# A diffusion trunk on one core: GpSimd's elementwise instructions go to VectorE

## The chip, the cores and the metric

The kernel runs on 1 core of one Trainium2 chip. The metric is device time in microseconds of one execution. Times before are given as the median of three runs. Engines: TensorE (PE, with PEld for its weight loads), VectorE (DVE), ScalarE (ACT), GpSimd (POOL) and SyncE (SP, here a queue for DMAs).

## The reference

Four layers over two streams of 256 tokens, a context (half 0) and a latent (half 1), D = 1024. The mixers are a gated linear attention (layers 0 and 3), a neighbourhood attention (layer 1) and an S5 state space (layer 2). Each layer does twice: norm, scale and shift by a vector computed from a condition, a mixer or a convolutional FFN, norm, scale, add to the residual. In the last layer only the latent goes on.

```python
for i in range(DEPTH):
    h = rmsnorm(x, norm_g[i, 0]) * (1.0 + m[1]) + m[0]
    x = x + m[2] * rmsnorm(mixer(h), norm_g[i, 1])
    h = rmsnorm(x, norm_g[i, 2]) * (1.0 + m[4]) + m[3]
    x = x + m[5] * rmsnorm(conv_ffn(h, ...), norm_g[i, 3])
```

## The kernel before

Activations lie transposed: eight tiles of 128 features (index k) by 256 tokens for each half. Matmuls are done in three passes over two parts of each operand: `mm3` (L688 to L690) multiplies the high part of the weights with the high and the low part of the input, and the low part of the weights with the high input. So each weight tile is split into `whi` (ScalarE, L112) and `wlo` (VectorE, L115), and each input into a high half (ScalarE, L574) and a low half, computed value minus high half.

There is no planner: each engine works off its instructions in the order in which the code emits them. Work beside the matmuls sits in Python generators that are advanced by `tick()` between matmuls; a `yield` in a generator sets what is emitted next. `drain()` runs all generators to their end with nothing in between.

**The step between stages** is `chain(l, n, half, nxt)`, called 14 times: after mixer (n = 1) or FFN (n = 3) of each layer, for each half. First it takes the square sums of y, which `sum_mm` (L446) broadcasts through a matmul with ones; `rstd_sb` takes the root on ScalarE (L460) and the reciprocal on VectorE (L462), named `bc`; in the last step `bc` is a ScalarE copy (L469) and `bp` the same values in PSUM, elsewhere both names are one SBUF tile. Then the residual loop over k: y times g times `bp` (L520, VectorE) and x plus y (L526, VectorE). For the k listed in `tp`, GpSimd has first multiplied y by `bc` (L517), and one VectorE instruction does the rest (L524). ScalarE squares the new x (L530) for the next norm. For the second half, and at the entry of S5, this loop is emitted in one burst; elsewhere it yields after each k.

After the second reciprocal the loop over k makes the next input: t = x times g times `bc` (L561, VectorE), the high half on ScalarE (L574), the low half on VectorE (L581), emitted with a delay of three entries (`HL`). For the k in `HP[half]` ScalarE writes the full value once more (L577) and GpSimd subtracts the high half (L578). This is done in 11 of the chains; at the entry of S5 there is no split.

**Square sums of the first half.** `sq_add` squares on ScalarE (L484). For half 0 `sq_sum` adds the squares of k = 2 to 6 elementwise onto two tiles (L476) so that fewer sums go through TensorE; k = 2 and 4 on GpSimd, the others on VectorE. After attention `outtail` copies y out of PSUM (L827 or L825) and calls `sq_add` for each of the eight tiles, with weight splits between; in the FFN the y tiles come one at a time (L980).

**S5 preparation.** `s5_prep` runs as a generator beside the FFN of layers 0 and 1, eight iterations each. Its `outer` makes two complex outer products: two products on VectorE (L1480), two on GpSimd into `Wt` (L1479), combined on VectorE (L1483, L1485); the result W goes to DRAM, or to TensorE for transposes (L1538). In front of the FFN's output, ScalarE and VectorE apply the convolution (L883, L886, L887), which frees the PSUM bank, and the gate (L892 to L895).

GpSimd's queue also issues the weight loads of the S5 mixer (L1555).

Of the kernel before, what the change touches and what calls it, by code (L numbers as in the profile page):

```python
# [19 lines left out]
FHEAD, FTAIL = (2, 1)  # L20
DM = 1
CW = (1, 8, 6)
HP = ((1, 3, 5), (1, 3, 5))
FT = (2, 6)
DF = 1
AE = (1, 1)
# [13 lines left out]
WB = 4  # L40
ORDER = '00 10 m 01 m f1 l 11 m 20 m 21 f2 30 m 31 m 40 f3 41 s 50 51 60 61 70 71'
TL = 1
TP = ((1, 3, 5, 7), (1, 3, 5, 7), (3, 6))
CF = (3, 2)
C0 = 3
ET = (0, 1)
# [24 lines left out]
MUL, ADD, SUB, MAX = ALU.mult, ALU.add, ALU.subtract, ALU.max  # L71
# [80 lines left out]
class Kern:  # L152
# [319 lines left out]
    def sq_sum(self, key, k, q):  # L472
        st = self.pst.setdefault(key, {})
        if 1 < k < 7:
            a = st[k % 2]
            (self.nc.vector if k % 2 or k == 6 else self.nc.gpsimd).tensor_tensor(a, a, q, op=ADD)  # L476
        else:
            st[k] = q

# [12 lines left out]
    def chain(self, l, n, half, nxt):  # L492
# [3 lines left out]
        if n is not None:  # L496
# [17 lines left out]
            g = lambda k: self.g1[:, l, n, k, half:half + 1]  # L514
            tp = TP[half if half or n == 1 and KINDS[l] != 2 else 2]
            for k in tp:
# [40 lines left out]
        for k in range(NK):  # L557
# [14 lines left out]
            else:  # L572
                hi, lo = self.hh[:, half, k], self.hl[:, half, k]
                nc.scalar.activation(hi, t, AF.Identity, bias=m, scale=1.0)  # L574
                if k in HP[half]:
                    h = self.np_.tile([128, 256], F32, name="sq", bufs=2)
# [882 lines left out]
    def s5_prep(self, p, i0, i1):  # L1459
        nc = self.nc  # L1460
# [11 lines left out]
        def outer(pw, br, bi, neg):  # L1472
            W = p.tile([128, 4, 2, 8, 16], F32, name="W", bufs=2)
            P = lambda i: pw[:, i, :, :, None].to_broadcast([128, 4, 8, 16])
            B = lambda x: x[:, :, None, :].to_broadcast([128, 4, 8, 16])
            v, g = nc.vector, nc.gpsimd
            for u, (x, y) in enumerate(((br, bi), (bi, br))):
                t = p.tile([128, 4, 8, 16], F32, name="Wt", bufs=1)
                g.tensor_tensor(t, P(1), B(y), op=MUL)  # L1479
                v.tensor_tensor(W[:, :, u], P(0), B(x), op=MUL)  # L1480
                yield
                if u and neg:
                    v.scalar_tensor_tensor(W[:, :, u], W[:, :, u], -1.0, t, op0=MUL, op1=SUB)  # L1483
                else:
                    v.tensor_tensor(W[:, :, u], W[:, :, u], t, op=ADD if u else SUB)  # L1485
            return W

        nxt = load(i0)
        for it in range(i0, i1):
# [10 lines left out]
            nc.vector.tensor_scalar(ncim, bc[:, 3, :4], -1.0, None, op0=MUL)  # L1500
            yield
            W = yield from outer(pw[:, 1], bc[:, 2, :4], bc[:, 3, :4], True)
            nc.sync.dma_start(self.Gd[it], W.rearrange("p g i s c -> p g i (s c)"))
            yield
            W2 = yield from outer(pw[:, 0], bb[:, 0, :4], bb[:, 1, :4], False)
            ps = self.aux()
            psb = self.aux()
# [25 lines left out]
            for h in range(2):  # L1533
                yield
                ps = self.aux()
                for u in range(4):
                    q, i = 2 * h + u // 2, u % 2
# [392 lines left out]
```

## Time and profile before

| | |
|---|---|
| median of three runs | 2921.64 us (2917.19 to 2922.3) |
| the profiled execution | 2920.22 us |
| its span, first to last instruction | 2918.4 us |
| mean granted TensorE clock | 0.969 |
| TensorE busy | 2740.2 us (94%) |
| VectorE busy | 1992.1 us (68%) |
| ScalarE busy | 1290.1 us (44%) |
| GpSimd busy | 194.9 us (7%), 192 instructions |

The span is what the profile covers; the metric holds 1.8 us more. Busy is the time in which an instruction of the engine was running; matmuls overlap, so TensorE's busy share isn't its share of its peak. The granted clock is 1.0 at 2.4 GHz and 0.5 at 1.2 GHz. An instruction's duration can overlap with that of the next one on its engine.

### The profile page before, as it was taken

How to read it: one execution, taken by the hardware profiler on the slowest of the kernel's cores; microseconds unless marked ns; L12 is line 12 of the kernel's file. 1: busy time of each engine (PE TensorE's matmuls, PEld its weight loads, DVE VectorE, ACT ScalarE, POOL GpSimd, SP SyncE). 2: the span in 40 equal slices, each digit the busy share in tenths (PEclk: the TensorE clock that was granted, in tenths of full speed). 3: DMA queues.
4: the chain of work that ended last, by engine and by line, in shares of the span. 5: the costliest groups of instructions: out<-in, count | busy, mean ns of one | idle time of the engine just before them, and what ended most of it. 6: DMA issues, size and time to landing. Idle time of an engine off the chain costs nothing.

```text
span 2918.4 us, 53174 instructions
## 1 busy us (share of the span) xinstructions
PE 2740.2 (94%) x21814; PEld 2267.2 (78%) x21814; DVE 1992.1 (68%) x4405; ACT 1290.1 (44%) x2154; POOL 194.9 (7%) x192
## 2 busy tenths in 40 slices
PE   8999998999999999899999877989999989998998
PEld 5787776877788777777777745778888877887998
DVE  5775768766557655687564766378687876777776
ACT  4333334634335545553333565454332463433554
POOL 0000001122101000012110010010000010000000
PEclk9999999999999999999999988899999999999999
DMA  6232232355524343235555387433334453332553
GB/s 260 88 112 93 102 99 76 131 178 178 172 93 150 104 164 109 102 123 191 199 180 178 125 228 251 150 120 132 137 124 147 143 179 126 120 124 95 186 182 124
DMA packets 127043, 421.26 MB, mean 144 GB/s; under 512 B 36048, under 2 KB 55760, under 8 KB 102096
## 3 DMA queue, kind: packets, MB, share of 16 engines
q1 hardware_dynamic: 118608, 391.64, 39.5%
q0 software_dynamic: 5472, 23.07, 2.3%
q8 instruction: 172, 2.82, 0.4%
q10 hardware_dynamic: 2720, 3.15, 0.3%
q14 instruction: 71, 0.58, 0.1%
HBM read 392.78 MB, written 29.23 MB: 145 GB/s over the span
## 4 chain that ended last, share of the span: by engine, by line
PE 72%; DVE 16%; ACT 5%; DMA 3%; issue 2%; SPq 1%; POOL 0%; ACTq 0%; DVEq 0%; POOLq 0%
PE acc L688 19%; PE acc L689 18%; PE acc L690 17%; DVE wlo L115 3%; PE aux L314 2%; PE aux L1103 2%; PE acc L724 2%; PE acc L726 1%; PE acc L725 1%; DVE bc L462 1%; DVE y L561 1%; ACT whi L112 1%; PE aux L1143 1%; PE aux L383 1%; DVE y L520 1%
## 5 line engine op out<-in xcount | busy, mean ns | idle before, releaser
L688 PE MATMUL acc<-h,whi 128*128 128x512 f32 (+1 forms) x2368 | 868.3, 367 | 24.8 <-ACT h L574 15.3
L689 PE MATMUL acc<-h,whi 128*128 128x512 f32 (+1 forms) x2368 | 842.7, 356 | 19.4 <-DVE h L581 17.0
L690 PE MATMUL acc<-h,wlo 128*128 128x512 f32 (+1 forms) x2368 | 837.8, 354 | 2.3 <-DVE wlo L115 2.3
L115 DVE TENSOR_TENSOR wlo<-wraw,whi 128x512 fp32r<-128x512 f32 (+5 forms) x674 | 601.7, 920 | 153.0 <-ACT whi L112 152.6
L688 PEld LDWEIGHTS acc<-h,whi 128*128 128x128 f32 x2368 | 458.6, 194 | 94.1 <-ACT h L574 18.2
L689 PEld LDWEIGHTS acc<-h,whi 128*128 128x128 f32 x2368 | 458.9, 194 | 80.0 <-DVE h L581 24.3
L112 ACT ACTIVATE whi<-wraw 128x1024 fp32r<-128x1024 f32 (+3 forms) x496 | 479.5, 1014 | 66.6 <-PE acc L689 51.7
L690 PEld LDWEIGHTS acc<-h,wlo 128*128 128x128 f32 x2368 | 458.8, 194 | 62.1 <-DVE wlo L115 3.2
L688 PE MATMUL acc<-gh,whi 128*128 128x256 f32 (+1 forms) x872 | 294.7, 338 | 8.6 <-ACT gh L894 8.6
L689 PE MATMUL acc<-gl,whi 128*128 128x256 f32 (+1 forms) x872 | 287.2, 329 | 0.8 <-DVE gl L895 0.7
L690 PE MATMUL acc<-gh,wlo 128*128 128x256 f32 (+1 forms) x872 | 287.1, 329 | 0.0
L883 ACT ACTIVATE u<-acc,vec 128x512 f32<-128x512 f32 (+1 forms) x190 | 129.6, 692 | 254.5 <-PE acc L690 254.3
L886 DVE SCALAR_TENSOR_TENSOR u<-acc,vec,u 128x510 f32<-128x510 f32 (+1 forms) x190 | 122.2, 643 | 113.2 <-ACT u L883 113.0
L688 PEld LDWEIGHTS acc<-gh,whi 128*128 128x128 f32 x872 | 164.8, 189 | 25.6 <-ACT gh L894 9.0
L689 PEld LDWEIGHTS acc<-gl,whi 128*128 128x128 f32 x872 | 164.7, 189 | 16.8 <-DVE gl L895 1.7
L690 PEld LDWEIGHTS acc<-gh,wlo 128*128 128x128 f32 x872 | 164.6, 189 | 15.9
L1074 DVE TENSOR_TENSOR FB<-FB,P 128x256 f32<-128x256 f32 x384 | 145.2, 421 | 31.9 <-PE aux L1103 29.3
L887 DVE SCALAR_TENSOR_TENSOR u<-acc,vec,u 128x510 f32<-128x510 f32 (+1 forms) x190 | 123.1, 648 | 6.7
L724 PE MATMUL acc<-whi,h 128*128 128x256 f32 x384 | 115.2, 300 | 2.2 <-ACT whi L112 1.2
L894 ACT ACTIVATE gh<-u 128x512 fp32r<-128x512 f32 (+1 forms) x95 | 52.3, 551 | 144.1 <-DVE u L893 144.1
L726 PE MATMUL acc<-wlo,h 128*128 128x256 f32 x384 | 110.0, 287 | 4.1 <-DVE wlo L115 4.1
L725 PE MATMUL acc<-whi,h 128*128 128x256 f32 x384 | 109.7, 286 | 0.0
(298 smaller groups left out, 3957.2 us busy)
## 6 DMA issues: line engine op xcount, KB each, us to landing
wm<-in_w_mod SPq DMA_DIRECT2D x192, 512.0 KB, 5.3
wraw<-in_f_w_in SPq DMA_DIRECT2D x89, 1024.0 KB, 4.9
wraw<-in_fo SPq DMA_DIRECT2D x44, 896.0 KB, 4.6
wraw<-in_a_qz SPq DMA_DIRECT2D x18, 1024.0 KB, 4.9
wraw<-in_a_zg SPq DMA_DIRECT2D x18, 1024.0 KB, 4.9
wraw<-in_fo SPq DMA_DIRECT2D x16, 1024.0 KB, 4.9
wraw<-in_a_v SPq DMA_DIRECT2D x15, 1024.0 KB, 4.9
wraw<-in_c_glu SPq DMA_DIRECT2D x12, 1024.0 KB, 4.8
```

Source lines behind the costliest of these rows:

```text
L112: nc.scalar.activation(hi[:, a:b], r[:, a:b], AF.Copy)
L115: nc.vector.tensor_tensor(lo[:, a:b], r[:, a:b], hi[:, a:b].bitcast(F32), op=SUB)
L688: nc.tensor.matmul(ps, wh[:, k], hh, start=(first and k == 0), stop=False, **kw)
L689: nc.tensor.matmul(ps, wh[:, k], hl, start=False, stop=False, **kw)
L690: nc.tensor.matmul(ps, wl[:, k], hh, start=False, stop=(last and k == nk - 1), **kw)
L724: nc.tensor.matmul(o, hh, wh[:, :, k, :], start=(k == 0), stop=False)
L725: nc.tensor.matmul(o, hl, wh[:, :, k, :], start=False, stop=False)
L726: nc.tensor.matmul(o, hh, wl[:, :, k, :], start=False, stop=(k == NK - 1))
L883: nc.scalar.activation(u, ps[c], AF.Identity, scale=w(1), bias=self.vec[:, cb0 + ch:cb0 + ch + 1])
L886: nc.vector.scalar_tensor_tensor(u3[:, :, 1:], p3[:, :, :255], w(0), u3[:, :, 1:], op0=MUL, op1=ADD)
L887: nc.vector.scalar_tensor_tensor(u3[:, :, :255], p3[:, :, 1:], w(2), u3[:, :, :255], op0=MUL, op1=ADD)
L1074: nc.vector.tensor_tensor(o, o, p, op=MUL)
```

## The change

All elementwise instructions of GpSimd go to VectorE. The lists `HP` and `TP` become empty: every low half is made by L581 (and ScalarE's second copy, L577, is not emitted), every residual product by L520 followed by L526. The square adds of k = 2 and 4 and the S5 products go to VectorE at the places in the code where GpSimd did them. GpSimd keeps its DMA issues and one memset. Nothing else is touched.

```diff
@@ -20,7 +20,7 @@
-HP = ((1, 3, 5), (1, 3, 5))
+HP = ((), ())
@@ -40,7 +40,7 @@
-TP = ((1, 3, 5, 7), (1, 3, 5, 7), (3, 6))
+TP = ((), (), ())
@@ -473,7 +473,7 @@
         if 1 < k < 7:
             a = st[k % 2]
-            (self.nc.vector if k % 2 or k == 6 else self.nc.gpsimd).tensor_tensor(a, a, q, op=ADD)
+            self.nc.vector.tensor_tensor(a, a, q, op=ADD)
         else:
             st[k] = q
@@ -1473,7 +1473,7 @@
             B = lambda x: x[:, :, None, :].to_broadcast([128, 4, 8, 16])
-            v, g = nc.vector, nc.gpsimd
+            v = g = nc.vector
             for u, (x, y) in enumerate(((br, bi), (bi, br))):
                 t = p.tile([128, 4, 8, 16], F32, name="Wt", bufs=1)
                 g.tensor_tensor(t, P(1), B(y), op=MUL)
```

## Rows read from the trace of the kernel before

**Rows 1.** The page: busy times, and the chain that ended last by engine.

```profile
PE 2740.2 (94%) x21814; PEld 2267.2 (78%) x21814; DVE 1992.1 (68%) x4405; ACT 1290.1 (44%) x2154; POOL 194.9 (7%) x192
...
PE 72%; DVE 16%; ACT 5%; DMA 3%; issue 2%; SPq 1%; POOL 0%; ACTq 0%; DVEq 0%; POOLq 0%
```

**Rows 2.** Groups by line, GpSimd: count | busy us, mean ns | idle before, releasers.

```profile
L1479 POOL TENSOR_TENSOR Wt<-pw,bb 128x512 f32<-128x512 f32 x32 | 46.7, 1459 | 100.3 <-DVE W L1485 61.0 <-DVE W L1483 39.3
...
L517 POOL TENSOR_TENSOR y<-y,bc 128x256 f32<-128x256 f32 x48 | 42.0, 902 | 611.5 <-DVE bc L462 407.8 <-ACT bc L469 203.6
L578 POOL TENSOR_TENSOR h<-sq,h 128x256 fp32r<-128x256 f32 x33 | 27.9, 846 | 160.6 <-ACT sq L577 160.1 <-POOL h L578 0.5
L476 POOL TENSOR_TENSOR sq<-sq,sq 128x256 f32<-128x256 f32 x12 | 10.4, 868 | 1383.2 <-ACT sq L484 1383.2
```

**Rows 3.** Durations of one line, L520: min/median/max ns.

```profile
L520 DVE SCALAR_TENSOR_TENSOR y<-y,g,bc x60: 470/478/1069, 473.9 to 2693.6; 128x256 f32<-128x256 f32 x60
```

**Rows 4.** Timeline, VectorE, 498 to 522 us: start, us, line, count.

```profile
498.38 2.50 DVE L115 TENSOR_TENSOR wlo<-wraw,whi 128x512 fp32r<-128x512 f32 x4 [0.34 <-ACT whi L112]
...
502.70 1.06 DVE L520 SCALAR_TENSOR_TENSOR y<-y,g,bc 128x256 f32<-128x256 f32 x1
...
508.87 0.48 DVE L524 SCALAR_TENSOR_TENSOR x<-y,g,x 128x256 f32<-128x256 f32 x1
...
513.96 1.67 DVE L561 SCALAR_TENSOR_TENSOR y<-x,g,bc 128x256 f32<-128x256 f32 x4
```

**Rows 5.** Timeline, GpSimd, the same stretch.

```profile
502.74 3.34 POOL L517 TENSOR_TENSOR y<-y,bc 128x256 f32<-128x256 f32 x4 [6.17 <-DVE bc L462]
```

**Rows 6.** Timelines, VectorE and TensorE, 2680 to 2712 us (layer 3).

```profile
2700.94 1.67 DVE L561 SCALAR_TENSOR_TENSOR y<-x,g,bc 128x256 f32<-128x256 f32 x4
...
2706.37 1.26 DVE L581 SCALAR_TENSOR_TENSOR h<-y,mT,h 128x256 fp32r<-128x256 f32 x3
...
2690.98 1.14 PE L446 MATMUL aux<-y,ones 128*128 128x256 f32 x2 [4.72 <-ACT y L530]
2692.71 5.85 PE L446 MATMUL aux<-y,ones 128*128 128x256 f32 x14 [0.59 <-ACT y L530]
...
2705.23 0.58 PE L689 MATMUL acc<-h,whi 128*128 128x256 f32 x1 [0.92 <-DVE h L581]
```

**Rows 7.** Timeline, VectorE, 1212 to 1275 us (after layer 1's attention).

```profile
1212.38 1.41 DVE L827 TENSOR_TENSOR y<-acc,y 128x256 f32<-128x256 f32 x4
1214.34 0.72 DVE L476 TENSOR_TENSOR sq<-sq,sq 128x256 f32<-128x256 f32 x1 [0.54 <-ACT sq L484]
```

**Rows 8.** Timelines, VectorE and TensorE, at the entry of S5.

```profile
1651.24 1.94 DVE L520 SCALAR_TENSOR_TENSOR y<-y,g,bc 128x256 f32<-128x256 f32 x2
...
1659.18 0.41 DVE L476 TENSOR_TENSOR y<-y 128x256 f32<-128x256 f32 x1
...
1663.94 0.58 PE L688 MATMUL acc<-gh,whi 128*128 128x256 f32 x1 [8.20 <-ACT gh L894]
```

**Rows 9.** Timeline, TensorE, in the S5 preparation: the longest wait for W.

```profile
588.00 0.55 PE L1538 MATMUL aux<-ident,W 128*128 128x128 f32 x3 [1.85 <-DVE W L1485]
```

**Rows 10.** Timeline, VectorE, the last residual step, first and last row.

```profile
2909.77 0.48 DVE L520 SCALAR_TENSOR_TENSOR y<-y,g,aux 128x256 f32<-128x256 f32 x1 [1.28 <-ACT bc L469]
...
2914.79 0.47 DVE L524 SCALAR_TENSOR_TENSOR x<-y,g,x 128x256 f32<-128x256 f32 x1
```

**Rows 11.** Timelines, TensorE, at transitions: waits that end on these steps.

```profile
506.86 3.82 PE L446 MATMUL aux<-y,ones 128*128 128x256 f32 x14 [1.03 <-ACT y L530]
...
904.60 0.70 PE L446 MATMUL aux<-sl,ones 128*128 128x256 f32 x2 [1.37 <-ACT sl L484]
...
1698.49 1.12 PE L1644 MATMUL acc<-ident,vt 128*64 128x128 f32 x8 [3.23 <-ACT vt L1637]
...
1922.81 0.39 PE L690 MATMUL acc<-h,wlo 128*128 128x256 f32 x1 [0.96 <-DVE wlo L115]
```

**Rows 12.** Stretches: us, busy us (count) by engine, PEclk, DMA share, GB/s.

```profile
560.00:740.00 180.00, 177.93 (x1154) 139.20 (x1153) 120.58 (x212) 69.84 (x109) 35.50 (x25) 0.99 0.51 174
```

## Prediction

> **What bounds the kernel now.** The page's busy times and its chain that ended last say that TensorE is the bound: 94% busy, 72% of the chain [rows 1]. VectorE has 16% of the chain, so more VectorE work can cost time, but only where TensorE waits for it. GpSimd has 0% of the chain and 7% of the span. Read alone, that says that its work is hidden and that moving it to a busier engine can only lose.
>
> The groups of instructions by line, GpSimd only, give the pieces that move [rows 2]: 64 S5 products at up to 1.46 us (two groups of 32; the longer stands), 48 residual products (902 ns), 33 low halves (846 ns) and 20 square adds (two groups; the twelve on the sq tiles stand, 868 ns). Next the durations of the VectorE line that does the same step as L517: 470 ns at least, 478 median, but 1069 at most [rows 3]. The timeline shows which are long. In the residual burst at 502 us GpSimd runs from 502.74 for 3.34 us [rows 5]; the VectorE instruction that starts at 502.70 takes 1.06 us and the one at 508.87, after GpSimd has ended, 0.48 [rows 4]. Both have the same size and both read two SBUF tensors. This is what the case turns on: while GpSimd computes, VectorE instructions there run at half speed. GpSimd has no time of its own on the chain, but it lengthens VectorE's.
>
> Last, TensorE's own idle times: which of them end on a chain of VectorE work. They stand at the transitions between stages [rows 6, 8, 9, 11, 12].
>
> **Prices.** From start to start a scalar_tensor_tensor of 128x256 takes (1.67 - 0.48)/3 = 0.40 us [rows 4]; a tensor_tensor (1.41 - 0.41)/3 = 0.33 us [rows 7, 8], both on data that GpSimd doesn't touch at that time; a tensor_tensor of 128x512 2.50/4 = 0.63 us at most [rows 4]. The last one of a run adds 0.08. The added low half, residual product and square add are such instructions, and the S5 product has the shape of the wlo row, with broadcast inputs; its bounds are 0.63 and, by GpSimd's row, 1.46 [rows 2], and I take 0.63, the same engine. VectorE gains 64 x 0.63 + 48 x 0.40 + 33 x 0.40 + 20 x 0.33 = 79 us of issue time; ScalarE loses 33 copies (L577, counted below at nothing, since VectorE paces those stretches).
>
> **A. Low halves (HP, 11 chains of three).** Before, VectorE issues 8 L561 and 5 L581; in layer 3 from 2700.94 to 2706.37 + 1.26 = 2707.63, so 6.69 us [rows 6]. After, 16 instructions without GpSimd: 16 x 0.40 + 0.08 = 6.4 us. The end gains 0.3, but TensorE waits earlier: it stood 0.92 us until 2705.23 for the low half of k=2 [rows 6]. In the code the order becomes t0 to t3, lo0, t4, lo1, t5, lo2, t6, lo3, t7, lo4. lo2 is the ninth instruction and ends 9 x 0.40 + 0.08 = 3.7 us after 2700.94; before, TensorE was released after 4.29. lo4 is the thirteenth, 5.3 us; before it was the first of the three at 2706.37 and ended after 5.9. So the halves that TensorE waits for come 0.6 sooner, and ScalarE's spared copies don't stand ahead of its own. I take 0.8 per chain, bounds 0.3 (the last half) and 1.3 (0.92 of idle and the 0.3): 11 x 0.8 = **8.8 us**, 3.3 to 14.
>
> **B. Residual bursts of the second half (TP, four products each).** Before: 502.70 to 508.87 + 0.48 = 6.65 us [rows 4], with 12 VectorE instructions. After: 8 x 0.40 + 8 x 0.33 + 0.08 = 5.9. Gain 0.73. TensorE waits for the squares of these rows (1.03 us at 506.86 [rows 11]) in three chains of this form: 2.2. In layer 3 the sums start 4.72 us late [rows 6]; row 0 is ready after two scalar_tensor_tensor and one tensor_tensor, 0.7 sooner, and row 1 sooner still by 1.7, so the 0.59 us before 2692.71 go as well: 1.3. At the entry of S5, TensorE waits 3.23 us for a ScalarE copy that stands behind those squares [rows 11]; up to 1.7, nothing if the S5 loads set the pace; I take 1.2. Two chains (near 935 and 2365 us) have other work between: 0 and 0.6. Sum **5.3 us**, 2 to 8.
>
> **C. Residual steps of the first half.** Entry of S5: one burst, 1651.24 to 1659.18 + 0.41 = 8.35 us, ending in TensorE's longest stall there, 8.20 us [rows 8]. After: 16 instructions and five adds, 8 x 0.40 + 13 x 0.33 + 0.08 = 7.6: 0.75. In the two FFN tails before layers 1 and 3 TensorE waits 1.37 us behind two L520 that take 1.94 together instead of 0.88 [rows 8, 11]: 0.7 each after the two added adds. At 1922.81 a wlo split stands behind such a pair, 0.96 us [rows 11]: 0.9.
> Against it: after attention, sq_add's adds come in VectorE's order between the copies of y. Each waits 0.54 us for its ScalarE square before it runs [rows 7]; two more such waits cost 2 x (0.54 + 0.33) = 1.7, less 2 x 0.3 for adds no longer slowed (0.72 there), so 1.1 late at the reciprocal, and the copies and weight splits behind them are late too. Then row 0 is ready 0.7 sooner, and the two products at k = 5 and 7 cost 2 x 0.40 where VectorE has no idle time. So 1.1 - 0.7 + 0.8 = 1.2 lost in each of two chains. In FFN tails TensorE is busy for longer than those waits: nothing; if that cover is gone, 8 adds x 0.87 = 7 us. Sum: 0.75 + 1.4 + 0.9 - 2.4 = **0.65 us**, -7 to 3.
>
> **D. The last residual step.** There bp is read from PSUM, and L520 isn't slowed (0.48). From 2909.77 to 2914.79 + 0.47 = 5.49 us [rows 10]; after 5.9. **0.4 us lost**, on the path to the last store.
>
> **E. S5 products.** They fall in the FFN stages of layers 0 and 1. In 560 to 740 us VectorE is busy 120.6 of 180 us and TensorE 177.9 [rows 12]. 25 of GpSimd's instructions there, at most 25 x 0.63 = 16 us more on VectorE, leave some 43 free. TensorE's stalls there are waits for W, the longest 1.85 us [rows 9], because VectorE waited for the product on GpSimd; with 0.63 in place of 1.46 this one and three shorter ones mostly go: **2 us**, 0 to 3.
>
> Sum: 8.8 + 5.3 + 0.65 - 0.4 + 2 = 16.3 us of the profiled execution's 2920.2 (span 2918.4, and 1.8 around it): 2903.9. That execution lies 1.4 us below the median, so 2905.3. The clock is taken as unchanged: the idle that lowers it between stages mostly stays.
>
> The burst of part B bears on a rule of the Trainium skill: four L561 take 1.67 us, though one lasts 0.48 [rows 4], so an instruction starts before the one before it has ended. "VectorE: DVE Perf Modes", section "The DRAIN you can't avoid", says that the next instruction doesn't start until the pipe is empty, though it allows an earlier start for one that isn't held. By the plain rule part B would lose and part A too; by the row both gain, and the row is of this kernel.
>
> **Rivals.**
> *Absorbed.* TensorE's sums, weight splits and ScalarE take the place of each wait. Then only the last halves (11 x 0.3), layer 3 (1.3), S5's burst (0.75) and half of E count: 6.4 - 0.4 - 2.4 = 3.6 us, 2918. For it: at the transitions TensorE also waits for ScalarE and weights. Against: the rows of 6, 8 and 11 end on exactly the slowed instructions. Within 0.2% (about 5.8 us, what a measurement of this kernel can tell from no change). 0.20.
> *VectorE becomes the bound in the S5 preparation (slower).* Each product sits in front of the convolution step that frees a PSUM bank. If every one held TensorE up by its 0.63: 64 x 0.63 = 40 us, and with A to D gaining 14, 2947. It decides from about 0.22 us per product. Against it: the 43 us free [rows 12], and four banks. 0.08; a typical case 2935.
> *Durations add up.* If added instructions cost their duration rather than the spacing, a burst takes 8 x 0.48 + 8 x 0.41 = 7.1 against 6.65, seven of them +3; the low halves 16 x 0.48 = 7.7 against 6.69, 11 x 1.0 = +11; D 7.1 - 5.49 = +1.6; C about +5 (the 2.4 stays, 0.8 at S5, 0.5 in each of three tails); E still -2: 19 us slower, 2940. The spacing rows speak against it. 0.06. (It is what the skill's rule named above would give.)
>
> **How the numbers follow.** Forecast 0.66, absorbed 0.20, the two slower cases 0.14. Likeliest 2905.3; its own range is 2894 (every upper bound at once, 28 us) to 2916 (where no change begins). The whole range, 2893 to 2923, takes in the absorbed case and leaves out the slower ones. Faster 0.66, same 0.20, slower 0.14.
>
> **What the profile after should show.** GpSimd left with the S5 loads alone; L520, L561, L581 and L526 without any at 0.9 us or more; the burst at about 5.9 us, the low halves at 6.4; TensorE's waits for low halves shorter, those for W nearly gone; the reciprocal after attention in layers 0 and 1 about 1 us late; the last step 0.4 longer. Wrong it would be if VectorE's instructions stay long without GpSimd, if they start only when the one before has ended, or if TensorE shows new waits for u or wlo in 560 to 740 us.

## The result, and the profile after

The changed kernel takes 2899.95 us (median of four runs, 2897.44 to 2904.39) against 2920.56 us for the kernel before beside it: ratio 0.9933, 95% interval 0.9919 to 0.9947, or 19.6 us less (15 to 24; the ratio is that of the means, the medians differ by 20.6). Forecast were 16.3 us less, 2905.3 us. The profiled execution has a span of 2898.8 us and a mean granted clock of 0.975.

The page after, with the lines of [rows 1]: busy times, and the chain by engine.

```profile
PE 2730.3 (94%) x21814; PEld 2255.8 (78%) x21814; DVE 2014.8 (70%) x4570; ACT 1281.6 (44%) x2121; POOL 15.5 (1%) x27
...
PE 71%; DVE 18%; ACT 5%; DMA 3%; issue 2%; SPq 1%; POOL 0%; ACTq 0%; DVEq 0%; POOLq 0%
```

VectorE executes 165 more instructions and is busy only 22.7 us longer. Issue time of 79 us was added, so the rest must have become shorter. Two views show it: the durations of L520 (ns, min/median/max), which answers to [rows 3], and the groups of VectorE by line and shape.

```profile
L520 DVE SCALAR_TENSOR_TENSOR y<-y,g,bc x104: 475/480/490, 476.6 to 2676.6; 128x256 f32<-128x256 f32 x104
```

```profile
L561 DVE SCALAR_TENSOR_TENSOR y<-x,g,bc 128x256 f32<-128x256 f32 x104 | 46.5, 480 | 1.1
L526 DVE TENSOR_TENSOR x<-x,y 128x256 f32<-128x256 f32 x112 | 46.4, 421 | 0.0
L581 DVE SCALAR_TENSOR_TENSOR h<-y,mT,h 128x256 fp32r<-128x256 f32 x88 | 39.6, 481 | 0.0
L476 DVE TENSOR_TENSOR sq<-sq,sq 128x256 f32<-128x256 f32 x30 | 12.8, 425 | 15.4 <-ACT sq L484 15.4
L1479 DVE TENSOR_TENSOR Wt<-pw,bb 128x512 f32<-128x512 f32 x32 | 22.1, 690 | 0.8
```

No residual or low-half instruction takes 0.9 us or more. The last two rows are moved work: an add that took 868 ns on GpSimd takes 425, a product that took 1459 takes 690 [rows 2].

VectorE's timeline has the residual burst of [rows 4] (first and last row), the low halves of layer 3 [rows 6] and the last residual step [rows 10].

```profile
504.16 0.88 DVE L520 SCALAR_TENSOR_TENSOR y<-y,g,bc 128x256 f32<-128x256 f32 x2
...
509.33 0.76 DVE L526 TENSOR_TENSOR x<-x,y 128x256 f32<-128x256 f32 x2
...
2682.51 1.67 DVE L561 SCALAR_TENSOR_TENSOR y<-x,g,bc 128x256 f32<-128x256 f32 x4
...
2687.27 1.67 DVE L581 SCALAR_TENSOR_TENSOR h<-y,mT,h 128x256 fp32r<-128x256 f32 x4
...
2889.80 0.87 DVE L520 SCALAR_TENSOR_TENSOR y<-y,g,aux 128x256 f32<-128x256 f32 x2 [1.28 <-ACT bc L469]
...
2894.94 0.76 DVE L526 TENSOR_TENSOR x<-x,y 128x256 f32<-128x256 f32 x2
```

The burst takes 5.93 us (forecast 5.9), the low halves 6.43 (6.4), the last step 5.90 (5.9). TensorE's timeline shows what it still waits for: in layer 3, at the entry of S5 and in the S5 preparation ([rows 6, 8, 9, 11] before).

```profile
579.05 0.62 PE L1510 MATMUL aux<-W,bb 64*32 64x112 f32 x24 [1.21 <-DVE W L1483]
...
587.30 0.55 PE L1538 MATMUL aux<-ident,W 128*128 128x128 f32 x3 [1.66 <-DVE W L1485]
...
1655.88 0.58 PE L688 MATMUL acc<-gh,whi 128*128 128x256 f32 x1 [8.02 <-ACT gh L894]
...
1689.00 0.66 PE L1644 MATMUL acc<-ident,vt 128*64 128x128 f32 x8 [1.58 <-ACT vt L1637]
...
2673.54 6.59 PE L446 MATMUL aux<-y,ones 128*128 128x256 f32 x16 [4.03 <-ACT y L530]
...
2686.21 0.58 PE L689 MATMUL acc<-h,whi 128*128 128x256 f32 x1 [0.17 <-DVE h L581]
```

The wait for the low half of k = 2 shrank from 0.92 to 0.17 us, and its matmul starts 3.70 us after the first L561 of the loop (4.29 before, forecast 3.7). Also shorter are the start of layer 3's sums, from 4.72 to 4.03, and the wait for vt, from 3.23 to 1.58. The 8.20 us stall lost only 0.18, and the waits for W stand.

**Where the 19.6 us came from.** Busy and idle time of TensorE (idle is span less busy), with a second profile of either kernel (below) in brackets: busy 2740.2 (2742.7) before and 2730.3 (2733.0) after, idle 178.2 (177.3) and 168.5 (166.5). In this account half of the gain is less idle time, and half is that the same 21814 matmuls took 10 us less. The number of matmuls is the same, so the second half is put down to the clock: its mean over the executions is 0.9680 in 43 of the kernel before (0.965 to 0.971) and 0.9722 in five of the changed one (0.970 to 0.975).

The account is not yet a price of the clock, since a TensorE that computes faster also waits more (last section). Executions at an equal clock tell more: with 0.970 or 0.971 the kernel before took 2915.3 us on average (eight executions, 2913.9 to 2917.2), the changed one 2900.3 (three, 2897.4 to 2904.4). So some 15 us of the gain are there without a higher clock, and about 5 go with it. With three executions on one side this is an estimate.

### The profile page after: what moved, and what is told of

It is laid out like the page before. It is cut to its first block, busy times and chain, and to the rows that moved or that the text cites. A ratio compares the mean times of both kernels' runs of the same rounds, so it can differ in the third digit from the quotient of the medians.

```text
span 2898.8 us, 52998 instructions
## 1 busy us (share of the span) xinstructions
PE 2730.3 (94%) x21814; PEld 2255.8 (78%) x21814; DVE 2014.8 (70%) x4570; ACT 1281.6 (44%) x2121; POOL 15.5 (1%) x27
## 4 chain that ended last, share of the span: by engine, by line
PE 71%; DVE 18%; ACT 5%; DMA 3%; issue 2%; SPq 1%; POOL 0%; ACTq 0%; DVEq 0%; POOLq 0%
PE acc L688 18%; PE acc L689 17%; PE acc L690 17%; DVE wlo L115 3%; PE aux L314 2%; PE aux L1103 2%; ACT whi L112 2%; PE acc L724 2%; PE acc L726 1%; PE acc L725 1%; DVE bc L462 1%; PE aux L1143 1%; PE aux L383 1%; DVE y L520 1%; DVE y L561 1%
## 5 line engine op out<-in xcount | busy, mean ns | idle before, releaser
L115 DVE TENSOR_TENSOR wlo<-wraw,whi 128x512 fp32r<-128x512 f32 (+5 forms) x674 | 591.2, 905 | 147.8 <-ACT whi L112 147.6
L688 PEld LDWEIGHTS acc<-h,whi 128*128 128x128 f32 x2368 | 453.6, 192 | 94.0 <-ACT h L574 19.1
L689 PEld LDWEIGHTS acc<-h,whi 128*128 128x128 f32 x2368 | 453.2, 191 | 73.0 <-DVE h L581 19.0
```

Of the source, the lines that this page charges most:

```text
L115: nc.vector.tensor_tensor(lo[:, a:b], r[:, a:b], hi[:, a:b].bitcast(F32), op=SUB)
L688: nc.tensor.matmul(ps, wh[:, k], hh, start=(first and k == 0), stop=False, **kw)
L689: nc.tensor.matmul(ps, wh[:, k], hl, start=False, stop=False, **kw)
```

## The experiments

**One part alone.** Theory: while a GpSimd instruction runs, VectorE's instructions with two SBUF inputs take twice as long, so every part that leaves GpSimd gains by itself. Rivals: other waits absorb it; one part is everything. Each kernel is the one before with one part of the change:

```diff
e1_low:  -HP = ((1, 3, 5), (1, 3, 5))
         +HP = ((), ())
e2_res:  -TP = ((1, 3, 5, 7), (1, 3, 5, 7), (3, 6))
         +TP = ((), (), ())
e3_sq:   -(self.nc.vector if k % 2 or k == 6 else self.nc.gpsimd).tensor_tensor(a, a, q, op=ADD)
         +self.nc.vector.tensor_tensor(a, a, q, op=ADD)
e4_s5:   -v, g = nc.vector, nc.gpsimd
         +v = g = nc.vector
```

> The kernel before with the low halves alone moved (HP empty, 33 of them, and ScalarE's 33 second copies gone); the residual products, square adds and S5 products stay on GpSimd. Theory (GpSimd's instructions lengthen VectorE's, so each part that takes them away gains by itself): 8.8 us less, 3.3 to 14. Rival 'absorbed' (TensorE's other waits take the place): about 3 us less. Rival 'one part carries all': nearly the whole 20.6 us or nothing.

> The kernel before with the residual products alone moved (TP empty, 48 of them). Theory: the bursts and residual steps gain 5.3 + 0.75 + 1.4 + 0.9 and lose 0.4, about 8 us less, of which up to 1.6 may be lost again where VectorE has no idle time after attention; 4 to 11. Timeline: the S5 entry should begin its first sums about 3.8 us sooner against its reciprocal, as it does with all parts moved. Rival 'absorbed': 2 us less or none.

> The kernel before with the 20 square adds alone moved. Theory: each moved add makes VectorE wait for its ScalarE square, so the reciprocals after attention in layers 0 and 1 come later; 2 us more in time (0 to 4). Rival (fewer GpSimd instructions always help): 1 to 2 us less, since the VectorE adds beside them are no longer slowed (0.72 down to 0.41 us).

> The kernel before with the 64 S5 products alone moved. Theory: 2 us less (0 to 3), by the waits for W and by the L115 splits and convolution steps that are no longer slowed. If the layer 0 FFN's gain of some 3 us and the loss of some 2 us in layer 1's FFN, which the two traces show between reciprocals, belong to these products, both show here without the other parts. Rival: the products hold TensorE up in the S5 preparation, 5 us more or worse.

| kernel | ratio to before (95%) | us | mean clock |
|---|---|---|---|
| e1_low | 0.9952 (0.9937 to 0.9967) | -14.0 | 0.9720 |
| e2_res | 0.9952 (0.9935 to 0.9969) | -14.0 | 0.9713 |
| e3_sq | 1.0002 (0.9992 to 1.0012) | +0.6 | 0.9694 |
| e4_s5 | 0.9995 (0.9986 to 1.0005) | -1.5 | 0.9701 |

Low halves and residual products carry the gain, each with more than was forecast for it. For square adds and S5 products no gain or loss can be told from none; the intervals also leave room for the 2 us that were forecast for either. One expectation fell: the gain of the layer 0 FFN is not that of the S5 products alone. Between the reciprocals (L462) at 512.11 and 899.69 us the changed kernel gains 3.1 us, e1_low 3.1, e2_res 2.7 and e4_s5 1.7.

**Both main parts, and ScalarE's copies.** The two gains add up to 28 us, more than the whole change has. e9_lowres is before with `HP` and `TP` empty. e8_copies tests what part A's gain is made of: the spared copies of L577 come back into the changed kernel, used by nobody.

```diff
                 nc.scalar.activation(hi, t, AF.Identity, bias=m, scale=1.0)
+                if k in (1, 3, 5):
+                    h = self.np_.tile([128, 256], F32, name="sq", bufs=2)
+                    nc.scalar.activation(h, t, AF.Identity, bias=m, scale=1.0)
```

> The kernel before with the low halves and the residual products moved (HP and TP empty), the square adds and the S5 products left on GpSimd. Alone these two parts gave ratios of 0.9952 each. Theory 'each gain is its own' (the stalls that each removes are different ones): ratio about 0.990, 28 us less, which beats the changed kernel by some 8 us, since square adds and S5 products gave nothing alone. Rival 'the two share a gain' (the profiles show that part of it is fewer stretches at 1.2 GHz, and one edit can be enough to keep the clock up): about 0.993, 20 us less, the same as the changed kernel.

> The changed kernel with ScalarE's 33 second copies (L577, k = 1, 3, 5 of each low-half loop) emitted again, used by nobody. Theory (VectorE paces the low halves, so the spared copies were worth nothing, as counted in the prediction): ratio stays near 0.993. Rival (part A's gain is that ScalarE's high halves come sooner because the copies don't stand ahead of them): about 8 us of the gain go, ratio near 0.996, and TensorE waits for high halves in those stages.

e9_lowres: 0.9933 (0.9921 to 0.9946), 2900.57 us, mean clock 0.9716. The rival holds: 0.990 lies outside the interval, and the two parts share a gain of 8 or 9 us. From the three intervals that shortfall is known only to 1 to 16 us (an estimate). e8_copies: 0.9943 (0.9931 to 0.9956), 2901.56 us; the rival's 8 us would be 0.9960, just above the interval, and losses up to 6 us are not excluded. TensorE's first wait for a high half in layer 3 is 2.46 us with and without the copies, so the trace gives the rival no support.

What is shared can be seen in the stretches (us, busy us and count by engine, PEclk, DMA share, GB/s) from 515 to 530, 900 to 985 and 1195 to 1275 us. First the kernel before in its second profile (e10_before), then the changed kernel; in the same stretch the kernels are up to 7 us apart in their work.

```profile
515.00:530.00 15.00, 13.57 (x100) 12.07 (x100) 13.26 (x27) 11.85 (x24) 2.47 (x3) 0.89 0.22 70
900.00:985.00 85.00, 75.81 (x496) 64.65 (x495) 59.81 (x109) 40.88 (x87) 12.36 (x14) 0.90 0.35 128
1195.00:1275.00 80.00, 67.49 (x422) 57.81 (x423) 65.63 (x122) 45.04 (x97) 13.27 (x16) 0.90 0.26 93
```

```profile
515.00:530.00 15.00, 14.30 (x117) 12.75 (x117) 13.38 (x32) 11.65 (x23) 0.00 (x0) 1.00 0.21 71
900.00:985.00 85.00, 77.31 (x537) 65.97 (x537) 62.14 (x132) 44.09 (x90) 0.00 (x0) 0.96 0.35 119
1195.00:1275.00 80.00, 69.55 (x464) 59.30 (x463) 63.34 (x129) 45.35 (x91) 0.00 (x0) 0.96 0.24 83
```

The same stretches in e1_low, and then in e2_res:

```profile
515.00:530.00 15.00, 14.31 (x118) 12.78 (x117) 13.27 (x32) 11.29 (x23) 0.00 (x0) 1.00 0.21 71
900.00:985.00 85.00, 76.39 (x530) 65.62 (x529) 62.61 (x123) 43.48 (x89) 7.12 (x8) 0.96 0.33 118
1195.00:1275.00 80.00, 68.34 (x467) 59.77 (x466) 64.69 (x121) 44.88 (x92) 8.39 (x10) 0.96 0.25 83
```

```profile
515.00:530.00 15.00, 13.61 (x110) 12.34 (x103) 13.37 (x27) 11.89 (x25) 2.52 (x3) 1.00 0.21 71
900.00:985.00 85.00, 76.10 (x515) 64.74 (x514) 59.88 (x119) 45.26 (x95) 7.78 (x8) 0.94 0.34 118
1195.00:1275.00 80.00, 69.11 (x461) 59.10 (x461) 63.43 (x123) 47.04 (x96) 6.38 (x8) 0.95 0.25 83
```

At 515 us the clock stays up if either part is done, and the second part can't raise it again. In the other two stretches either part alone lifts it from 0.90 to between 0.94 and 0.96, where the changed kernel has 0.96 (0.94 and 0.98 in its second profile). At 515 us e2_res still has the waits for low halves (0.45 and 0.57 us by TensorE's timeline) and yet keeps 1.00. Where it falls is seen in e10_before, TensorE:

```profile
925.64 0.39 PE L689 MATMUL acc<-h,whi 128*128 128x256 f32 x1 [0.66 <-DVE h L581]
...
927.79 0.58 PE L689 MATMUL acc<-h,whi 128*128 128x256 f32 x1 [0.93 <-DVE h L581]
928.16 0.41 PE L690 MATMUL acc<-h,wlo 128*128 128x256 f32 x1
928.38 0.41 PE L688 MATMUL acc<-h,whi 128*128 128x256 f32 x1
928.59 0.42 PE L689 MATMUL acc<-h,whi 128*128 128x256 f32 x1
```

After waits of 0.62, 0.66 and 0.93 us, the last of which ended 3.2 us after the first, each matmul takes 0.21 us from start to start instead of 0.12: 1.2 instead of 2.4 GHz. The changed kernel's profile shows 0.61, 0.66 and 0.51, then three waits of 0.17 to 0.18 us there, and the matmuls stay at 0.12.

**GpSimd runs, and nobody needs it.** These two tell contention apart from waiting for GpSimd's results. Both are the changed kernel, with useless work on GpSimd beside the residual loops (48 places), the low halves (33) and the square adds (20); VectorE never waits for it. The S5 products have no such counterpart, and line numbers behind the new function are 6 and 8 higher (L526 and L528 are L520, L532 is L526).

```diff
e6_dummy, and e7_memset with the lines of the second half instead:
+    def idle(self, src):
+        gd = self.np_.tile([128, 256], F32, name="gd", bufs=1)
+        self.nc.gpsimd.tensor_tensor(gd, src, src, op=MUL)

+        self.nc.gpsimd.tensor_copy(gd[:, :1], src[:, :1])
+        for _ in range(3):
+            self.nc.gpsimd.memset(gd, 0.0)
```

> The changed kernel, with GpSimd computing products that nobody uses (128x256, reading SBUF) at the same places as before: 48 beside the residual loops, 33 beside the low halves, 20 beside the square adds; VectorE waits for none of them. Theory (a running GpSimd instruction halves the speed of VectorE's two-input instructions): instructions of 0.9 to 1.1 us are back on L520, L526, L561 and L581, and the time goes back to that of the kernel before or above it, ratio 0.998 to 1.008. Rival (what was lost was VectorE's wait for GpSimd's results and the hand-over between the engines): L520 and L561 stay at 0.48 us, ratio stays near 0.993.

> As the run with unused products, but each replaced by three memsets of 128x256 on GpSimd (about 0.8 us together, an estimate from the memset rows of the trace), which write SBUF and read nothing, with a copy of one column ahead that waits for the same tile. Theory, by the Trainium skill, page SBUF — State Buffer, section Who interferes with whom (only a GpSimd instruction that reads SBUF holds VectorE up): durations stay at 0.48 us and the ratio near 0.993. Rival (any running GpSimd instruction that touches SBUF slows VectorE): as with the products, ratio 0.998 or more.

e6_dummy: ratio 1.0067 (1.0053 to 1.0080), 2937.12 us. e7_memset: 0.9935 (0.9923 to 0.9948), 2899.98 us. First e6_dummy, VectorE in the burst that ran in 5.93 us above, and GpSimd beside it; then the durations of e6_dummy's and of e7_memset's copy of L520.

```profile
507.74 1.24 DVE L526 SCALAR_TENSOR_TENSOR y<-y,g,bc 128x256 f32<-128x256 f32 x2
508.90 0.83 DVE L532 TENSOR_TENSOR x<-x,y 128x256 f32<-128x256 f32 x1
509.65 0.83 DVE L526 SCALAR_TENSOR_TENSOR y<-y,g,bc 128x256 f32<-128x256 f32 x1
510.41 0.83 DVE L532 TENSOR_TENSOR x<-x,y 128x256 f32<-128x256 f32 x1
511.16 0.47 DVE L526 SCALAR_TENSOR_TENSOR y<-y,g,bc 128x256 f32<-128x256 f32 x1
```

```profile
507.85 3.10 POOL L474 TENSOR_TENSOR gd<-bc 128x256 f32<-128x256 f32 x4 [7.11 <-DVE bc L462]
```

```profile
L526 DVE SCALAR_TENSOR_TENSOR y<-y,g,bc x104: 468/476/840, 477.3 to 2711.6; 128x256 f32<-128x256 f32 x104
```

```profile
L528 DVE SCALAR_TENSOR_TENSOR y<-y,g,bc x104: 474/479/487, 474.4 to 2676.3; 128x256 f32<-128x256 f32 x104
```

Long instructions are back, with 0.83 us here and 0.90 at most on the four lines (0.9 to 1.1 were expected), and end with GpSimd's last product at 510.95. VectorE is busy 2049.4 us, 34.6 more than after for the same 4570 instructions, which is 0.34 us for each of the 101 products. The span is 36.2 us longer, and the clock in the three stretches above is back at 0.89 to 0.90. e7_memset keeps GpSimd busy for longer (172.1 us against 93.4) and changes nothing. So what was lost was not the wait for a result, and not that GpSimd runs or writes SBUF. What the products do and the memsets don't is to read SBUF. The Trainium skill, page "SBUF — State Buffer", section "Who interferes with whom", says the same: a VectorE instruction with two SBUF inputs contends with a GpSimd instruction that reads SBUF, and not with one that only writes it. The trace agrees in the bursts (0.83 against 0.42 us); in the last step of e6_dummy it doesn't (last section).

**Second profiles, and the square adds back.** e10_before and e11_after repeat the two kernels without an edit. e5_sqback is the changed kernel with the line of e3_sq as it was before.

> The kernel before once more, unchanged, for a second profile. The two profiles differ in TensorE's mean granted clock, 0.969 before and 0.975 after. Theory (the change removes stalls, and the clock falls less often as a consequence): the clock comes out at 0.968 to 0.971 again, TensorE's busy time at 2738 to 2742 us. Rival (where the clock falls differs from one execution to the next by as much as between the kernels): clock up to 0.975, busy time down to 2730.

> The changed kernel once more, unchanged, for a second profile. Theory (fewer low-clock stretches belong to the change): clock 0.974 to 0.976, TensorE's busy time about 2730 us, idle about 168. Rival (chance): clock down to 0.970, busy time up to 2738, with idle time smaller by as much, since a TensorE that computes slower waits less.

> The changed kernel with the square adds of k = 2 and 4 back on GpSimd, nothing else. Theory (on VectorE each of them waits for its ScalarE square, which makes the reciprocals after attention late): the reciprocals at 475 and 1218 us come 1 to 2 us sooner against the work before them, and the time is 2 us less, ratio 0.992 to 0.993. Rival (GpSimd's adds slow the weight splits and y's residual steps beside them by as much): 2 us more, ratio 0.994.

e10_before: 2921.81 us, clock 0.967. e11_after: 2901.51 us, clock 0.974. Both lie nearer to their own kernel's first profile than to the other's, although e10_before falls just below the 0.968 that was expected. By the means the kernel decides on the clock more than chance does, but single executions scatter by 0.0015 to 0.002, and two of e3_sq reach 0.973 and 0.974, so one profile can't show it. e5_sqback: 0.9927 (0.9914 to 0.9941), 2898.23 us, which is not told apart from the changed kernel; in the trace the place is plain. VectorE of the changed kernel, then of e5_sqback, from the last reciprocal of the attention (L426) to that of the chain (L462):

```profile
460.29 0.17 DVE L426 RECIPROCAL rs<-rs 128x2 f32<-128x2 f32 x1 [0.47 <-ACT rs L425]
...
464.31 0.42 DVE L476 TENSOR_TENSOR sq<-sq,sq 128x256 f32<-128x256 f32 x1 [0.48 <-ACT sq L484]
...
474.86 1.75 DVE L462 RECIPROCAL bc<-aux 128x256 f32<-128x256 f32 x1
```

```profile
458.67 0.17 DVE L426 RECIPROCAL rs<-rs 128x2 f32<-128x2 f32 x1 [0.48 <-ACT rs L425]
459.40 0.56 DVE L115 TENSOR_TENSOR wlo<-wraw,whi 128x384 fp32r<-128x384 f32 x1 [0.57 <-ACT whi L112]
459.88 1.41 DVE L827 TENSOR_TENSOR y<-acc,y 128x256 f32<-128x256 f32 x4
...
471.66 1.75 DVE L462 RECIPROCAL bc<-aux 128x256 f32<-128x256 f32 x1
```

It is 14.57 us with the adds on VectorE and 12.99 with them on GpSimd (12.99 in the kernel before, too): 1.58 us late. After layer 1's attention (L1275 to L462) it is 22.80 against 21.52: 1.28.

## Why the prediction was right

**The main reason** held: GpSimd had no time of its own on the chain and lengthened VectorE's, and e6_dummy and e7_memset show it by direct trial. The prices of 0.40 and 0.33 us from start to start held as well, so that burst, low halves and last step came out within 0.05 us.

**A and B** were the right places; measured alone, each gave more than its term. With C's gains less the part of its losses that belongs to the products (0.1 for each of two chains) and less D, the residual products were to give 7.75 us; alone they gave 14.0 (9 to 19). The low halves were to give 8.8, at most 14, and gave 14.0 (10 to 18). The reason is the step "The clock is taken as unchanged: the idle that lowers it between stages mostly stays". It failed. Either part raises the mean clock from 0.968 to 0.971 or 0.972; 0.004 are 2 x 0.004 x 2900 = 23 us less at half speed, worth at most half of that, 12 us; by the executions at an equal clock it is less, about 5. Both together raise it no further (0.9716), and the sum of the two falls short by the 8 or 9 us of e9_lowres. Measured together A, B, C's gains and D are 19.6 us, forecast 16.55. That either part alone keeps the clock up is shown for the three stretches. Over the whole span it is argued, from the means and from executions at an equal clock: with 0.970, e1_low and e2_res are each 5.9 us below the 2915.3 of before (two executions each), and e9_lowres, with 0.970 and 0.971, is 14.6 below. There nothing of the sum is missing, as far as so few executions can tell.

TensorE's idle time fell by 10 us, where A to E are 16.3; but idle time grows when TensorE computes faster, and at an equal clock the gain is some 15 us, near the sum. That the total came within 3.3 us is in part luck: the clock, which the sum has at nothing, added about 5, and E's 2 us are not seen. The wait for vt shows how waiting and clock mix: it fell by 1.65 us (forecast 1.2), and the matmul group behind it takes 0.66 us instead of 1.12 [rows 11], since the clock is up. The entry of S5 gave 3.8 us between its reciprocals (L462 at 1692.28 and 1711.13 before), in e2_res too, but the stretch behind it, to the reciprocal at 1917.55, became 1.3 to 2.9 us longer, measured against the two profiles of before; up to there 0.8 to 2.5 us are left, around the 1.2 forecast. Layer 3 gave 1.7 and 2.7 in the two profiles (forecast 1.3).

**C.** Three of its four gains came about as forecast: from the reciprocals at 899.69 and 2324.37 to the next ones 0.93 us each (0.7), from the one at 1917.55 on 0.61 (0.9). (The pair of 1.94 us that is shown is the one at the entry of S5 [rows 8]; the trace has the same at 901.49.) The square adds cost 1.6 and 1.3 us after attention (forecast 1.1). The products at k = 5 and 7 cost nothing in layer 0: from that reciprocal to the next one the changed kernel gains 1.1 us in both profiles, where a loss of 0.1 stood, so this chain ends with 0.4 lost and not with 1.2. In layer 1 it gains 1.3 and 2.4, but the two profiles of before differ by 1.3 there, which settles nothing. The burst at the entry of S5 takes 7.61 us (forecast 7.6), but of the 0.75 only 0.18 shows in the stall there, and 0.39 or 0.40 in e2_res and e9_lowres, whose square adds stay on GpSimd. In the FFN of layer 1 (reciprocals 1265.03 to 1649.46 before) the changed kernel loses 1.6 and 0.7 us in its two profiles, e4_s5 1.5 and e3_sq 0.8, while e9_lowres gains 0.9. "Nothing" for square adds and products in the FFN was therefore about 1 us too good. Part of it is the square adds: at the end of this FFN TensorE of the changed kernel waits for the square sums.

```profile
1639.29 0.70 PE L446 MATMUL aux<-bc,ones 128*128 128x256 f32 x2 [0.36 <-ACT bc L484]
```

The wait is there in both profiles of the changed kernel (0.36, 0.38) and in e3_sq (0.57), and in none of the two of before, e2_res, e9_lowres and e5_sqback, where the adds stay on GpSimd. So "in FFN tails TensorE is busy for longer than those waits" failed here. Two profiles of before differ by 0.5 us over this FFN, so what the products add stays open.

**D** cost 0.4 us, as forecast. **E** can't be told from nothing (e4_s5: 1.5 us less, between 4 less and 1.5 more), where 2 us were taken. The sentence that the waits for W "mostly go" failed: the longest is 1.66 us after 1.85, and a new one of 1.21 stands at 579.05. The new one is not the products' alone, since e9_lowres, with the products on GpSimd, has 0.85 us there. VectorE makes these products in half of GpSimd's time, but one after the other with its own two and behind its weight splits; that this is why the waits stand is argued from the order in the code and not tested.

**The rivals.** *Absorbed* is refuted by its size. *VectorE becomes the bound* would have shown in e4_s5. *Durations add up* needed a burst of 7.1 us; it takes 5.93.

No version beat the changed kernel by more than can be measured: e5_sqback and e9_lowres tie with it, so moving square adds and S5 products neither helps nor hurts by an amount that these runs can tell.

## What to carry to other kernels

An engine with no share of the chain can still set its pace: compare the durations of one instruction on the busy engine with and without the idle one beside it, before its work is called hidden. Moving elementwise work from GpSimd to a VectorE that is 70% busy paid, because VectorE does it in half the time and gets its own speed back. When two edits both shorten waits of TensorE, don't add their gains before both have been measured together: here the part that goes with a clock that stays up seems to be paid once.

## What the hardware showed unexpectedly

The price of contention is 0.34 us per GpSimd product on average (which lasts about 0.77), and it need not come at all. In e6_dummy's first burst above, four products make 5.93 us into 7.49; in its last step 5.90 become 5.98. In that last step the products run from 2926.07 for 3.07 us, and the adds beside them, which read two SBUF tensors, take 0.42 to 0.44 us, against 0.83 in its first burst. VectorE there alternates them with L526 reading PSUM (0.47). The traces don't show why these adds are spared. VectorE's rows, and last GpSimd's:

```profile
2925.96 0.87 DVE L526 SCALAR_TENSOR_TENSOR y<-y,g,aux 128x256 f32<-128x256 f32 x2 [1.34 <-ACT bc L469]
2926.75 0.42 DVE L532 TENSOR_TENSOR x<-x,y 128x256 f32<-128x256 f32 x1
...
2927.47 0.44 DVE L532 TENSOR_TENSOR x<-x,y 128x256 f32<-128x256 f32 x1
...
2926.07 3.07 POOL L474 TENSOR_TENSOR gd<-bc 128x256 f32<-128x256 f32 x4 [203.16 <-ACT bc L469]
```

Slower matmuls and waiting trade places: e7_memset, e8_copies and e9_lowres have spans within 0.5 us (2896.1 to 2896.6) with TensorE busy for 2726.0, 2733.6 and 2735.6 us. Busy time and idle time of one profile should therefore be read together.
